# Shift and scale vectors of the first layer in quarters of 256 channels, x loaded ahead of the context

## The chip, the cores and the metric

The kernel runs on one core of one Trainium2 chip. The metric is the device time of one execution in microseconds (us), the median of several runs. Engines: TensorE (PE, matmuls; PEld, its weight loads), VectorE (DVE), ScalarE (ACT), GpSimd (POOL), and SP, which here only issues DMA transfers.

## What is computed

One hybrid layer (attention beside a Mamba-2 scan), one short-convolution layer, each followed by a SwiGLU, over 512 latent tokens `x` with 1024 channels, and 256 context tokens `ctx` that only layer 0 reads. All of it is float32. What matters here is the entry into layer 0:

```python
mod = (jax.nn.silu(c) @ ada_w[0] + ada_b[0])[:, None, :]
sh1, sc1, g1, sh2, sc2, g2 = jnp.split(mod, 6, axis=-1)
hx = modulate(rms_norm(x, norm_mix[0]), sh1, sc1)          # h * (1 + scale) + shift
mod_c = (jax.nn.silu(c_ctx) @ ada_w[0] + ada_b[0])[None, None, :]
csh1, csc1, ... = jnp.split(mod_c, 6, axis=-1)
hc = modulate(rms_norm(ctx, norm_mix[0]), csh1, csc1)
p_lat, p_ctx = hx @ w_in, hc @ w_in                        # keys, values, queries, ...
```

So the kernel needs, before any projection, the first two of the six parts of `ada_w[0]` (shift and scale, 1024 columns each, 8 MB together), for two vectors, `c` and `c_ctx`.

## The kernel before, in words

Activations lie with channels on the partitions: `xt` is 128 x 8 x 512, chunk k holding channels 128k to 128k+127. Every large product is made of three matmuls (`mm3`, lines 114 to 120) on values split into a high and a low half: `split` (line 92) lets ScalarE round to the high half and VectorE subtract for the low one.

`hybrid` (line 339) is the start. `load` issues ctx and x, two transfers each. `begin` makes the sums of squares (`stats`: squares on ScalarE, adds on GpSimd for ctx and VectorE for x, then matmuls with ones), the reciprocal root (`rsqrt`, nine small operations on VectorE), its broadcast over the partitions (`bcast`, matmuls, line 307) and the product with every chunk (line 366: GpSimd for ctx, VectorE for x). `both` on line 359 sets which of the two goes first.

`ada_first` (line 206) makes shift and scale with matmuls that fill only 32 of the array's columns each, four of them side by side ("strips", lines 198 to 204). It runs over four groups, each for one part and one half of the channels: shift of half 0, scale of half 0, shift of half 1, scale of half 1. Each group loads four tiles `adaw` of 512 KB, makes 16 strip matmuls into a `psS` tile, copies the result out on ScalarE (`strip_r`, line 222), and turns it by two matmuls with the constant `pick` (line 224) into columns; VectorE adds the bias (lines 228, 229) and, after a scale group, makes `gsc` and `cgsc` (lines 232, 233). Then the generator yields the half, and `hybrid` makes that half's four chunks (lines 382 to 384): ScalarE writes the high half `act_hi` or `hc_hi`, VectorE the full value `mod_u`, and VectorE (x) or GpSimd (ctx) the low half `act_lo` or `hc_lo`.

`jobs` runs `begin` after the first transfer of the first group and `weights` after the first transfer of the third group; `weights` issues and splits the first three tiles of the plan, the kv weights `w_kvd`.

`mixer` (line 388) then projects keys, values and dt (the kv matmuls, lines 406 to 415): for every chunk k six token groups, 0 and 1 of ctx, accumulated in one `psS` tile (`kvc`), 2 to 5 of x, in three `psA` tiles and one `psV` tile. 8 x 6 x 3 = 144 matmuls of 272 columns. The q projection follows (lines 429 to 437, 96 matmuls of 512 columns), then ten feature tiles, the rotary work and the masks on VectorE and GpSimd.

A planner orders each engine's instructions by priority and by its own idea of when they become ready; an engine then runs its list in order. `manual_schedule` holds an engine to the written order inside the block. `psS` has two buffers, `psA` three, `psV` one; `adaw` twelve; the weight tiles `wst`, `whi`, `wlo` three each.

## Time and profile before

| | us |
|---|---|
| median of 3 runs (lowest, highest) | 1289.33 (1287.85, 1292.81) |
| the profiled execution | 1291.26 |
| its span, first to last instruction | 1289.4 |
| TensorE busy in it | 1239.6 (96%) |
| VectorE busy | 729.4 (57%) |
| ScalarE busy | 448.4 (35%) |
| GpSimd busy | 179.5 (14%) |
| data moved by DMA | 158.52 MB, mean 123 GB/s |

A busy share is an average over the whole span. What a change at the start is worth is read from the first hundred microseconds: which wait ends last there. The chain of work that ended last is 83% TensorE.

### The profile page before, as it was taken

Reading aid. Unit: us, or ns where it says so; the run is one execution under the profiler, and the core shown is the slowest. Engines: PE = TensorE matmul, PEld = TensorE weight load, DVE = VectorE, ACT = ScalarE, POOL = GpSimd, SP = SyncE. Lnnn points to the kernel's source line nnn. Section 1 sums busy time; section 2 is a strip of 40 time slices with the busy share of each in tenths; the row PEclk is TensorE's granted clock in tenths of the full one; section 3 lists DMA queues with packets and bytes.
Section 4 is the critical chain, followed back from the end, with each engine's and each line's share of the span. In section 5 each row is a group of like instructions: output and inputs, shape, how many; then the busy total and the mean of one; then the engine's idle time right before and its main releaser. Section 6 shows DMA issues by size and latency. Waiting matters only on the chain.

```text
span 1289.4 us, 15875 instructions
## 1 busy us (share of the span) xinstructions
PE 1239.6 (96%) x6086; PEld 1021.6 (79%) x6086; DVE 729.4 (57%) x1187; ACT 448.4 (35%) x675; POOL 179.5 (14%) x199
## 2 busy tenths in 40 slices
PE   5998988899999999999999999999999999999997
PEld 3887765567898888888888988888988888888886
DVE  4898799985564777788422554443743333332223
ACT  3534534455353222223222342223532222222221
POOL 3423335440220000000000100002200000000001
PEclk9999989999999999999999999999999999999998
DMA  9331343300514777777333323333133333333322
GB/s 369 127 99 49 96 155 125 115 17 1 163 50 143 227 243 243 235 240 249 118 91 94 111 79 93 95 97 112 50 114 98 99 98 98 97 91 90 94 87 66
DMA packets 54845, 158.52 MB, mean 123 GB/s; under 512 B 6000, under 2 KB 8688, under 8 KB 54512
## 3 DMA queue, kind: packets, MB, share of 16 engines
q1 hardware_dynamic: 54480, 157.20, 38.1%
q8 instruction: 48, 0.79, 0.2%
q10 hardware_dynamic: 288, 0.31, 0.1%
q14 instruction: 29, 0.24, 0.1%
HBM read 154.86 MB, written 2.10 MB: 122 GB/s over the span
## 4 chain that ended last, share of the span: by engine, by line
PE 83%; DVE 9%; DMA 3%; issue 3%; POOL 1%; ACT 0%; SPq 0%; DVEq 0%; ACTq 0%; POOLq 0%
PE psS L116 14%; PE psS L117 14%; PE psS L118 14%; PE psA L116 10%; PE psA L118 10%; PE psA L117 10%; DVE xtok L257 2%; PE psV L830 2%; DMA adaw<-ada 2%; PE psS L961 1%; PE psS L822 1%; DVE mx L804 1%; DVE wlo L95 1%; PE psS L963 1%; DMA xT<-xT 1%
## 5 line engine op out<-in xcount | busy, mean ns | idle before, releaser
L95 DVE TENSOR_TENSOR wlo<-wst,whi 128x1024 fp32r<-128x1024 f32 (+2 forms) x194 | 235.0, 1214 | 315.2 <-ACT whi L94 312.3
L94 ACT CAST whi<-wst 128x1024 fp32r<-128x1024 f32 (+2 forms) x194 | 198.2, 1025 | 544.8 <-PE psS L117 242.1
L116 PE MATMUL psS<-act_hi,whi 128*128 128x512 f32 x760 | 297.0, 391 | 1.2 <-DVE cs_a L573 1.0
L117 PE MATMUL psS<-act_lo,whi 128*128 128x512 f32 x760 | 296.7, 390 | 0.0
L118 PE MATMUL psS<-act_hi,wlo 128*128 128x512 f32 x760 | 296.6, 390 | 0.0
L118 PEld LDWEIGHTS psS<-act_hi,wlo 128*128 128x128 f32 x760 | 143.1, 188 | 29.7
L116 PEld LDWEIGHTS psS<-act_hi,whi 128*128 128x128 f32 x760 | 143.0, 188 | 29.5 <-issue 1.2
L117 PEld LDWEIGHTS psS<-act_lo,whi 128*128 128x128 f32 x760 | 143.0, 188 | 27.9
L325 POOL TENSOR_TENSOR sq_acc<-sq_acc,sq 128x512 f32<-128x512 f32 (+1 forms) x28 | 38.0, 1356 | 872.5 <-issue 645.8
L116 PE MATMUL psA<-ffn_h_hi,whi 128*128 128x512 f32 (+1 forms) x396 | 145.3, 367 | 0.0
L118 PE MATMUL psA<-ffn_h_hi,wlo 128*128 128x512 f32 (+1 forms) x396 | 144.9, 366 | 0.0
L117 PE MATMUL psA<-ffn_h_lo,whi 128*128 128x512 f32 (+1 forms) x396 | 144.8, 366 | 0.0
L257 DVE SCALAR_TENSOR_TENSOR ada_acc<-ada_st,silu_c,ada_acc 128x512 f32<-128x512 f32 x98 | 73.4, 749 | 27.5 <-DMA ada_st<-ada 26.0
L117 PEld LDWEIGHTS psA<-ffn_h_lo,whi 128*128 128x128 f32 x396 | 74.7, 189 | 12.1
L116 PEld LDWEIGHTS psA<-ffn_h_hi,whi 128*128 128x128 f32 x396 | 74.7, 189 | 12.0
L118 PEld LDWEIGHTS psA<-ffn_h_hi,wlo 128*128 128x128 f32 x396 | 74.7, 189 | 12.0
L116 PE MATMUL psA<-act_hi,whi 128*128 128x512 f32 (+1 forms) x216 | 80.0, 370 | 0.0
L118 PE MATMUL psA<-act_hi,wlo 128*128 128x512 f32 (+1 forms) x216 | 79.2, 367 | 0.8 <-DVE wlo L95 0.8
L117 PE MATMUL psA<-act_lo,whi 128*128 128x512 f32 (+1 forms) x216 | 79.5, 368 | 0.0
L916 DVE SCALAR_TENSOR_TENSOR xT<-psA,mod,xT 128x512 f32<-128x512 f32 (+1 forms) x40 | 25.7, 643 | 68.2 <-PE psA L118 68.0
L94 ACT CAST ffn_h_hi<-sg 128x512 fp32r<-128x512 f32 x44 | 27.4, 622 | 59.1 <-DVE sg L980 59.1
L118 PEld LDWEIGHTS psA<-act_hi,wlo 128*128 128x128 f32 x216 | 40.8, 189 | 8.0 <-DVE wlo L95 1.3
(297 smaller groups left out, 1804.4 us busy)
## 6 DMA issues: line engine op xcount, KB each, us to landing
wst<-w_gu SPq DMA_DIRECT2D x88, 512.0 KB, 3.6
ada_st<-ada SPq DMA_DIRECT2D x112, 256.0 KB, 4.0
wst<-w_dn SPq DMA_DIRECT2D x32, 512.0 KB, 3.5
wst<-ada SPq DMA_DIRECT2D x24, 512.0 KB, 3.8
wst<-w_sc SPq DMA_DIRECT2D x24, 512.0 KB, 3.6
adaw<-ada SPq DMA_DIRECT2D x16, 512.0 KB, 10.4
wst<-w_dn SPq DMA_DIRECT2D x16, 384.0 KB, 3.2
wst<-w_f SPq DMA_DIRECT2D x10, 512.0 KB, 3.6
```

What stands on the lines that cost most here:

```text
L94: nc.scalar.copy(hi, src)
L95: nc.vector.tensor_tensor(lo, src, hi.bitcast(F32), ALU.subtract)
L116: nc.tensor.matmul(out, lhsT=a[0], rhs=b[0], start=start, stop=False)
L117: nc.tensor.matmul(out, lhsT=a[0], rhs=b[1], start=False, stop=False)
L118: nc.tensor.matmul(out, lhsT=a[1], rhs=b[0], start=False, stop=stop)
L257: nc.vector.scalar_tensor_tensor(a, w[:, i], c, a, ALU.mult, ALU.add)
L325: nc.gpsimd.tensor_tensor(self.acc[:, ts], self.acc[:, ts], sq, ALU.add)
L804: nc.vector.tensor_reduce(mx[:, c:c + 1], s[:, 0:768], AX.X, ALU.max)
L822: nc.tensor.matmul(s[:, a * T:a * T + T], lhsT=kt[x][:, ks], rhs=q[x], start=(x == 0), stop=(x == 1))
L830: nc.tensor.matmul(av, lhsT=vz[:, kc, vs], rhs=e[:, a], start=(c + a == 0), stop=(c + a == CHUNKS - 1))
L916: nc.vector.scalar_tensor_tensor(xt[:, d, ts], ps, gate[:, d:d + 1], xt[:, d, ts], ALU.mult, ALU.add)
L961: nc.tensor.matmul(out, lhsT=a[:, k * P:(k + 1) * P], rhs=hi, start=(k == 0 and a is w[0]), stop=False)
```

## The change

`ada_first` now runs over eight groups, each for one part and one quarter (256 channels, two chunks). A group loads two tiles of 512 KB from a new input `ada_first`, which holds the same weights in another layout, four chunks of the inner dimension by 256 columns each. The four strips now stand for four chunks of the inner dimension instead of two chunks by two column halves, so `pick` has two columns and adds four strips up. The strip matmuls are held to the written order on TensorE. After each scale group a quarter is yielded, and its two chunks are made.

Further: x comes before ctx in `both`, in `load` and in the kv matmuls' inner loop; the three kv weights are issued one by one, after the groups 1, 3 and 5; and SP is held to the written order until the last chunk is made.

```diff
@@ -195,43 +195,39 @@
     def psS(self):
         return self.ps.tile([P, 1024], F32, name="psS", tag="S", bufs=2)
 
-    def strips(self, ps, w, lhsT, first, last):
-
-        for i in range(2):
-            for h in range(2):
-                g = 32 * (2 * i + h)
-                self.nc.tensor.matmul(ps[g:g + 32, 0:256], lhsT=lhsT[i], rhs=w[:, i, 256 * h:256 * h + 256],
-                                      start=first, stop=last)
-
     def ada_first(self, pool, jobs):
+
         nc, t = self.nc, self.t
         scw = pool.tile([P, KC, 2, 16], F32, name="silu_w")
         for v in range(2):
             nc.vector.tensor_copy(scw[:, :, v, :], self.sc[:, v, :, None].broadcast_to([P, KC, 16]))
         scw = scw.rearrange("p k v r -> p k (v r)")
-        for n, j in enumerate((0, 2, 1, 3)):
-            part, half = j // 2, j % 2
+        for n in range(8):
+            quarter, part = n // 2, n % 2
             ps = self.psS()[:, 0:512]
-            for q in range(4):
-                w = pool.tile([P, 2, 512], F32, name="adaw", tag="adaw", bufs=12)
-                nc.sync.dma_start(out=w, in_=t["ada"][0, j, :, 2 * q:2 * q + 2, :])
-                if (n, q) in jobs:
-                    jobs[n, q]()
-                self.strips(ps, w, [scw[:, 2 * q + i] for i in range(2)], q == 0, q == 3)
+            for e in range(2):
+                w = pool.tile([P, 4, 256], F32, name="adaw", tag="adaw", bufs=12)
+                nc.sync.dma_start(out=w, in_=t["ada_first"][part, quarter, e])
+                if (n, e) in jobs:
+                    jobs[n, e]()
+                with self.tc.manual_schedule(engines={mybir.EngineType.PE}):
+                    for i in range(4):
+                        nc.tensor.matmul(ps[32 * i:32 * i + 32, 0:256], lhsT=scw[:, 4 * e + i], rhs=w[:, i],
+                                         start=(e == 0), stop=(e == 1))
             r = pool.tile([P, 256], F32, name="strip_r", tag="strip_r", bufs=2)
             nc.scalar.copy(r, ps[:, 0:256])
             for x in range(2):
-                nc.tensor.matmul(ps[:, 256 + x:264:2], lhsT=r[:, x * P:(x + 1) * P], rhs=self.con("pick", 4),
+                nc.tensor.matmul(ps[:, 256 + 2 * x:258 + 2 * x], lhsT=r[:, x * P:(x + 1) * P], rhs=self.con("pick", 2),
                                  start=True, stop=True)
-            hs = slice(4 * half, 4 * half + 4)
-            b = self.vec("ada_b", 4 * j, 4)
-            nc.vector.tensor_tensor(self.mod[:, 0, part, hs], ps[:, 256:260], b, ALU.add)
-            nc.vector.tensor_tensor(self.cmod[:, part, hs], ps[:, 260:264], b, ALU.add)
+            ks = slice(2 * quarter, 2 * quarter + 2)
+            b = self.vec("ada_b", 8 * part + 2 * quarter, 2)
+            nc.vector.tensor_tensor(self.mod[:, 0, part, ks], ps[:, 256:260:2], b, ALU.add)
+            nc.vector.tensor_tensor(self.cmod[:, part, ks], ps[:, 257:260:2], b, ALU.add)
             if part == 1:
-                g = self.vec("norm_mix", 4 * half, 4)
-                nc.vector.scalar_tensor_tensor(self.gsc[:, 0, 0, hs], self.mod[:, 0, 1, hs], 1.0, g, ALU.add, ALU.mult)
-                nc.vector.scalar_tensor_tensor(self.cgsc[:, hs], self.cmod[:, 1, hs], 1.0, g, ALU.add, ALU.mult)
-                yield half
+                g = self.vec("norm_mix", 2 * quarter, 2)
+                nc.vector.scalar_tensor_tensor(self.gsc[:, 0, 0, ks], self.mod[:, 0, 1, ks], 1.0, g, ALU.add, ALU.mult)
+                nc.vector.scalar_tensor_tensor(self.cgsc[:, ks], self.cmod[:, 1, ks], 1.0, g, ALU.add, ALU.mult)
+                yield quarter
 
     def ada_rest(self, pool, layer, parts, acc=None, bufs=2, tag=None):
         nc, t = self.nc, self.t
@@ -356,7 +352,7 @@
                 nc.scalar.copy(rb, self.bcast(r, n // P)[0])
                 return rb
 
-            both = ((ct, TC, nc.gpsimd), (xt, T, nc.vector))
+            both = ((xt, T, nc.vector), (ct, TC, nc.gpsimd))
 
             def begin():
                 rows = [self.stats(sp, a, n, eng=eng) for a, n, eng in both]
@@ -366,13 +362,14 @@
                         eng.tensor_tensor(a[:, k], a[:, k], rb, ALU.mult)
 
             def weights():
-                for i in range(3):
-                    self.ready.append(self.weight(*self.plan[i]))
-
+                self.ready.append(self.weight(*self.plan[len(self.ready)]))
+
+            order = tc.manual_schedule(engines={mybir.EngineType.SP})
+            order.__enter__()
+            load(xt, "xT")
             load(ct, "ctxT")
-            load(xt, "xT")
-            for half in self.ada_first(sp, {(0, 0): begin, (2, 0): weights}):
-                for k in range(4 * half, 4 * half + 4):
+            for quarter in self.ada_first(sp, {(0, 0): begin, (1, 1): weights, (3, 1): weights, (5, 1): weights}):
+                for k in range(2 * quarter, 2 * quarter + 2):
                     for a, n, eng in both:
                         x = a is xt
                         g, s = (self.gsc[:, 0, 0], self.mod[:, 0, 0]) if x else (self.cgsc, self.cmod[:, 0])
@@ -382,6 +379,7 @@
                         nc.scalar.activation(hi, halved(a[:, k]), AF.Identity, bias=s[:, k:k + 1], scale=g[:, k:k + 1])
                         nc.vector.tensor_scalar(u, a[:, k], g[:, k:k + 1], s[:, k:k + 1], ALU.mult, ALU.add)
                         eng.tensor_tensor(lo, halved(u), hi.bitcast(F32), ALU.subtract)
+            order.__exit__(None, None, None)
         with tc.tile_pool(name="mix", bufs=1) as mp:
             return self.mixer(mp, h, hc, hcp)
 
@@ -411,7 +409,7 @@
             wv = [a[:, :544].rearrange("p (a b) -> p a b", a=2) for a in w]
             for i in range(2):
                 k = 2 * q + i
-                for c in range(CHUNKS):
+                for c in (2, 3, 4, 5, 0, 1):
                     self.mm3(kv[c], hc.tok(k, c) if c < 2 else h.tok(k, c - 2), [wv[0][:, i], wv[1][:, i]], k == 0, k == KC - 1)
         ssk = pp.tile([P, CHUNKS, 2], F32, name="ssk")
         ssq = pp.tile([P, 4, 8], F32, name="ssq")
@@ -1092,6 +1090,8 @@
     s = f["sc_w_in"][0]
     a["w_sc"] = np.stack([_tiles(s[:, q * D:(q + 1) * D], P) for q in range(3)], axis=1)
     a["w_so"] = _tiles(f["sc_w_out"][0], P)
+    first = f["ada_w"][0][:, :2 * D].reshape(2, 4, P, 2, 4, 256)
+    a["ada_first"] = first.transpose(3, 4, 0, 2, 1, 5)
     a["ada"] = np.stack([_tiles(f["ada_w"][l], 512) for l in range(2)])
     parts = [_cols(f["c"]), _cols(f["c_ctx"]), _cols(f["ada_b"]), _cols(f["norm_mix"]), _cols(f["norm_ffn"]),
              _cols(f["final_norm"]), _cols(f["hy_conv_w"][0]), _cols(f["hy_conv_b"]),
@@ -1107,9 +1107,8 @@
     con[:, 0:128] = np.eye(P)
     con[:, 128:256] = 1.0
     con[:, 256:384] = q[:, None] % 32 == q[None, :] % 32
-    for g in range(4):
-        for v in range(2):
-            con[32 * g + 16 * v, 384 + 2 * v + g % 2] = 1.0
+    for v in range(2):
+        con[16 * v::32, 384 + v] = 1.0
     at = CAT[1]
     con[:, at:at + 128] = le
     con[:, at + 128:at + 256] = ge
```

## Rows read from the trace of the kernel before

**Rows 1.** The page: busy tenths in 40 slices of 32.2 us, granted clock, DMA share

```profile
PE   5998988899999999999999999999999999999997
DVE  4898799985564777788422554443743333332223
PEclk9999989999999999999999999999999999999998
DMA  9331343300514777777333323333133333333322
```

**Rows 2.** Stretches: us; busy us (instructions) per engine; PEclk, DMA share, GB/s

```profile
7.00:21.00 14.00, 8.07 (x43) 6.26 (x44) 6.76 (x22) 6.80 (x14) 4.05 (x6) 1.00 1.02 415
21.00:35.40 14.40, 12.03 (x120) 6.23 (x119) 10.62 (x27) 4.78 (x10) 6.00 (x8) 1.00 1.02 393
36.40:39.80 3.40, 3.40 (x21) 2.35 (x21) 3.40 (x7) 2.94 (x6) 3.21 (x3) 0.60 0.42 170
39.80:57.10 17.30, 17.30 (x141) 16.73 (x140) 14.77 (x28) 8.57 (x15) 8.54 (x9) 1.00 0.18 52
57.10:79.10 22.00, 22.00 (x98) 17.89 (x97) 19.95 (x72) 7.48 (x19) 4.08 (x8) 1.00 0.41 123
52.70:101.10 48.40, 45.09 (x239) 38.18 (x237) 45.21 (x117) 17.94 (x37) 19.68 (x24) 0.99 0.31 95
101.10:104.60 3.50, 3.43 (x12) 2.96 (x13) 3.50 (x4) 0.90 (x2) 3.50 (x4) 0.59 0.00 0
104.60:160.00 55.40, 53.24 (x277) 43.03 (x276) 41.03 (x80) 27.51 (x55) 16.63 (x33) 1.00 0.27 78
```

**Rows 3.** Timeline of SP: start, us, queue, line, transfer, count

```profile
2.77 11.54 SPq L217 DMA_DIRECT2D adaw<-ada  x9
...
15.26 2.89 SPq L108 DMA_DIRECT2D wst<-w_kvd  x3
19.10 7.02 SPq L217 DMA_DIRECT2D adaw<-ada  x7
```

**Rows 4.** DMA issues at 1.65 and near 25.8 us: size, us to landing

```profile
xT<-xT SPq DMA_DIRECT2D x1, 1024.0 KB, 8.5
...
adaw<-ada SPq DMA_DIRECT2D x1, 512.0 KB, 10.8
```

**Rows 5.** Timeline of VectorE, 20 to 53 us: start, us, what, count, [idle before]

```profile
22.16 0.67 DVE L150 SCALAR_TENSOR_TENSOR rs_y<-rs_t,rs_y 128x4 f32<-128x4 f32 x1
...
27.70 5.16 DVE L366 TENSOR_TENSOR xT<-xT,rb 128x512 f32<-128x512 f32 x8
...
34.23 0.16 DVE L232 SCALAR_TENSOR_TENSOR gsc<-mod,vecs 128x4 f32<-128x4 f32 x1
...
44.72 0.16 DVE L232 SCALAR_TENSOR_TENSOR gsc<-mod,vecs 128x4 f32<-128x4 f32 x1
...
50.80 1.82 DVE L384 TENSOR_TENSOR act_lo<-mod_u,act_hi 128x512 fp32r<-128x512 f32 x2
```

**Rows 6.** Timeline of TensorE: x's broadcast, first q matmul, two waits near 100 us

```profile
25.11 1.32 PE L307 MATMUL psA<-cons,rs_y 128*128 128x128 f32 x8
...
57.11 0.40 PE L116 MATMUL psS<-whi,act_hi 128*128 128x512 f32 x1
...
99.48 0.66 PE L584 MATMUL psA<-cons,xf 128*128 128x128 f32 x4 [2.22 <-DVE xf L576]
101.17 0.76 PE L116 MATMUL psS<-act_hi,whi 128*128 128x512 f32 x1 [1.03 <-DVE cs_a L573]
```

**Rows 7.** Timeline of GpSimd: the normalisation of ctx

```profile
22.09 6.00 POOL L366 TENSOR_TENSOR ctxT<-ctxT,rb 128x256 f32<-128x256 f32 x8 [10.64 <-ACT rb L356]
```

**Rows 8.** Groups on GpSimd, 36 to 53 us: busy us, mean ns, idle before

```profile
L384 POOL TENSOR_TENSOR hc_lo<-mod_u,hc_hi 128x256 fp32r<-128x256 f32 x8 | 8.6, 1095 | 14.8 <-ACT hc_hi L382 14.5 <-DVE mod_u L383 0.3
```

**Rows 9.** Instructions on tile mod_u, 30 to 55 us: ns min/median/max, first and last start

```profile
L383 DVE TENSOR_SCALAR mod_u<-xT,gsc,mod x8: 535/542/959, 34.4 to 49.9; 128x512 f32<-128x512 f32 x8
...
L384 DVE TENSOR_TENSOR act_lo<-mod_u,act_hi x8: 679/884/1217, 36.9 to 51.9; 128x512 fp32r<-128x512 f32 x8
```

## The prediction

> **What bounds the kernel now.** I read the forty slices first [rows 1]. TensorE stands at nine tenths almost everywhere; the two places to look at are the first slice, where it does little and the DMA engines are full, and the stretch up to slice 9, where VectorE is at seven to nine tenths beside it. The change touches only what happens before the q projection, so I then read the early stretches one by one [rows 2]. From 7 to 35.4 us the DMA share is 1.02 at 393 to 415 GB/s: transfers bound this part. From 39.8 to 57.1 us TensorE is busy for all 17.3 us while DMA falls to 0.18: now the key and value (kv) matmuls bound. They could not start sooner, because the first scale vector (`gsc`) comes at 34.23 and the second at 44.72 [rows 5], each for half of the channels. The first q matmul is at 57.11 [rows 6]. From there to 101.1 VectorE is nearly full too (45.21 of 48.4 us between 52.7 and 101.1, rows of [rows 2]), and twice it holds TensorE up, 2.22 and 1.03 us [rows 6], after which the clock row falls to 0.59.
>
> So the end of the whole kernel moves by what the q projection's start moves, as far as VectorE lets it through. I work out the end of the kv matmuls, now 57.1.
>
> **The change, part by part.**
>
> *Quarters in place of halves.* The bytes are the same: sixteen transfers of 512 KB, with x, ctx and three kv weights among them. The last of the seven late ones is issued near 25.8 us (19.10 + 7.02 less its own issue) and lands 10.8 us later, at 36.5 [rows 3, 4]. I keep 36.5. The first quarter needs only four of the sixteen, so the first two kv chunks can start some 12 us before 35.4, and the last quarter holds back only two chunks of eight. In before, `gsc` trails the last landing by 8.2 us (36.5 to 44.72), since strips, copy and picks stand in order behind matmuls and VectorE work. Its bare work is about 2.3 us, an estimate from eight strips, a copy, two picks and four small adds of 0.16 us [rows 5]. Behind `gsc` came 7.9 us for four chunks (44.72 to 52.62, the end of the last `act_lo`) [rows 5], so 4.0 for two. Then TensorE's tail: 36 matmuls at most, at 17.30/141 = 0.123 us each [rows 2] 4.4 us, of which about half run beside VectorE: 2.2. The **DMA chain** thus ends between 36.5 + 2.3 + 4.0 + 2.2 = 45.0 and 50.9.
>
> *x ahead of ctx.* The first half of x lands at 10.2 (issued 1.65, 8.5 us) [rows 4]. Without ctx's 1 MB ahead of it that is 2.5 us earlier at 415 GB/s [rows 2]. Its broadcast now waits on TensorE from 22.83 to 25.11 behind strips [rows 5, 6]; if x's statistics lead, these 2.3 us go too. So x's normalisation starts not at 27.70 but at about 22.9; without the queue gain it is 25.2. ctx pays: its rows come after x's on ScalarE and VectorE, and GpSimd owes it 6.0 us of normalising and 8.6 us of `hc_lo` [rows 7, 8]. If its root (1.8 us) follows x's eight products (5.2 us) on VectorE, it starts near 30 instead of 22.09 and ends near 44.6, still ahead of VectorE below. The ctx accumulators also share the two buffers of `psS` with the eight strip groups, so ctx matmuls may queue until the seventh group is read, near 39; 36 + 36 matmuls at 0.123 us then end near 48. The new chunk order (x chunks first) lets TensorE do x meanwhile and costs nothing by itself.
>
> *VectorE, the real limit of the start.* From 27.70 to 52.62 it was busy 22.4 us (24.9 less the 2.5 idle in 39.8 to 57.1) [rows 2, 5]. Added are eight more small adds and four more products, 12 x 0.16 = 1.9 us at most; ctx's reciprocal root, nine small operations, may now fall into this time, 1.8 us; the first kv weight's split, 1.1 us. Part of this fits into the idle time before 23 us (VectorE was busy 6.76 of 14 us there [rows 2]); I charge about half, 2.3 of the 4.8. So VectorE ends at 22.9 + 22.4 + 2.3 = 47.6, with TensorE's last matmuls 1.9 behind: **49.5**. The durations hide a spread: the same `mod_u` took 0.535 to 0.959 us and `act_lo` 0.679 to 1.217 [rows 9], the long ones where GpSimd worked too. With all sixteen short, 9.7 us, with all long, 17.4; the medians' 11.4 lie nearer the short end. [...]
>
> *More instructions elsewhere.* Four more copies of the strips on ScalarE, and eight more picks of about 0.15 us on TensorE, 1.2 us: hidden under the transfers before 36 us, except the last pair, which is in the 2.3. If the cover went, they cost those 1.2 us. The strips themselves stay 64 matmuls of 256 columns.
>
> *Fixed order on SP.* In before the SP queue already issues ctx, x, nine strips' weights, three kv weights, seven more [rows 3], which is the written order, so this edit alone gives 0. Queued behind a waiting transfer would be the next kv weight and all later transfers; the thirteenth transfer needs the first of twelve buffers back, which its strips free long before. A later weight cannot overtake, and none has to.
>
> **What is late next.** The q projection starts 57.1 - 49.5 = 7.6 us earlier. It lasts 22.0 us on TensorE [rows 2], unchanged. VectorE has 19.95 us of work there, and in 52.7 to 101.1 only 3.2 us idle, so it gains 5.0 us (52.6 to 47.6) against TensorE's 7.6. The missing 2.6 us can come from work that nobody awaits yet: after 104.6 VectorE is idle 14.4 of 55.4 us [rows 2]. As the planner orders each engine by what is ready, I expect that to be moved and the gain to pass.
>
> **Sum.** The profiled execution took 1291.3 us, a span of 1289.4 and 1.9 around it; less 7.6 that is 1283.7. The median of the three runs is 1.9 lower, 1289.3, and on it the forecast is **1281.7**. The bounds are 45.0, and 49.5 + 2.3 = 51.8 where x's normalisation starts at 25.2: a gain of 5.3 to 12 us.
>
> **The rivals.**
>
> *Everything hidden, chance 0.15.* VectorE gets the short durations, the DMA chain binds: 45.0, a gain of 12, and the 3.3 us of waits near 100 us shrink too. That gives 1274 to 1278, say 1276. For it: VectorE idles half the time from 7 to 21 us. Against it: strips stood in line 8.2 us in before.
>
> *VectorE keeps the difference, 0.14.* If the idle work is not moved, TensorE gains only what VectorE gains, 3.1 (47.6 plus the 1.9 behind it) to 5.0 us: about 1285.5. For it: 45.21 busy of 48.4, and both waits near 100 us have VectorE as releaser.
>
> *GpSimd beside VectorE, 0.06.* ctx's 14.6 us on GpSimd now lie wholly beside x's sixteen operations. If all of these take their long times, VectorE ends 6.0 us later and the gain is 1.6: 1287.7. Against it: GpSimd worked beside most of them in before, and the medians are as they are. [...]
>
> [...]
>
> *ctx becomes the tail, slower, 0.08.* ctx's reciprocal root stands behind x's eight products and the first chunks on VectorE. From the normalisation of ctx on, GpSimd needs 14.6 us, and a few matmuls follow, 1.5 us. The point where it decides is 57.1 - 16.1 = 41: each microsecond that ctx starts later is lost. Started at 48, with x's later operations stuck behind ctx's on VectorE, it costs 7: 1296. Against it: nine operations of 0.2 us have to be late by 18 us over my 30.
>
> *It does not do what it says, 0.01.* The bytes before the last quarter are the same, and if the first quarters' kv matmuls wait in TensorE's order behind the last strips, nothing moves: 1289.
>
> **How the numbers follow.** The forecast case, 1279.5 to 1284.5, has 0.50. A measurement of this kernel tells about 0.5%, 6.4 us, from no change, so the line is 1282.9. Of the forecast's 0.50 three quarters lie below it, 0.37; with the hidden case's 0.15 that is faster 0.52. Same is 0.13 + 0.14 + 0.06 + 0.06 + 0.01 = 0.40. Slower is 0.08. The range runs from 1276 to 1288: it leaves out the slower case, half of the best one and part of the clock's.
>
> **What would show it.** The first kv matmul near 23 us instead of 35.4; x's normalisation near 23; the last `gsc` between 39 and 43; the last `act_lo` near 47.6; the first q matmul near 49.5; the waits near 100 us about 7 us earlier. [...]

## The result, and the profile after

The kernel after takes 1299.03 us (median of eight executions, 1294.36 to 1300.46) against 1291.38 us for the kernel before beside it: a ratio of 1.0058, 95% interval 1.0040 to 1.0077, slower by 0.6%. The forecast was 1281.7. The profiled execution of after took 1300.46 us, a span of 1298.7 where before had 1289.4. It is the slowest of the eight, so the 9.3 us between the spans are more than the 7.7 between the medians. What follows splits the 9.3 us, and three marks in the timeline of SP show where they arise: the first `cdup` transfer (the conv part is through), the first `w_gu` transfer (the mixer is nearly through), and the end.

The timeline of SP in before (start, us, queue, line, transfer):

```profile
143.46 2.44 SPq L701 DMA_DIRECT2D cdup<-cf  x4
340.87 9.50 SPq L108 DMA_DIRECT2D wst<-w_gu  x4
```

and in after:

```profile
147.47 2.44 SPq L699 DMA_DIRECT2D cdup<-cf  x4
350.26 9.59 SPq L108 DMA_DIRECT2D wst<-w_gu  x4
```

`cdup` is 4.0 us later, `w_gu` 9.4, and from there to the end both take the same (948.5 and 948.4 us). So **4.0 us are lost up to `cdup`**, in and behind the start that the change rewrites, and **5.4 more in the mixer's attention and SSD part**, where not a line was changed.

**The start.** VectorE's timeline in after, 24 to 55 us (start, us, line, what), against [rows 5]:

```profile
24.19 0.16 DVE L224 TENSOR_TENSOR mod<-psS,vecs 128x2 f32<-128x2 f32 x1 [1.93 <-PE psS L220]
24.27 7.01 DVE L362 TENSOR_TENSOR xT<-xT,rb 128x512 f32<-128x512 f32 x8
31.20 0.14 DVE L225 TENSOR_TENSOR cmod<-psS,vecs 128x2 f32<-128x2 f32 x1
...
32.38 0.68 DVE L228 SCALAR_TENSOR_TENSOR gsc<-mod,vecs 128x2 f32<-128x2 f32 x1
...
38.54 0.16 DVE L228 SCALAR_TENSOR_TENSOR gsc<-mod,vecs 128x2 f32<-128x2 f32 x1
...
44.37 0.16 DVE L224 TENSOR_TENSOR mod<-psS,vecs 128x2 f32<-128x2 f32 x1 [2.79 <-PE psS L220]
...
45.01 0.16 DVE L228 SCALAR_TENSOR_TENSOR gsc<-mod,vecs 128x2 f32<-128x2 f32 x1
...
50.33 0.16 DVE L224 TENSOR_TENSOR mod<-psS,vecs 128x2 f32<-128x2 f32 x1 [2.27 <-PE psS L220]
...
51.35 0.16 DVE L228 SCALAR_TENSOR_TENSOR gsc<-mod,vecs 128x2 f32<-128x2 f32 x1
...
53.11 1.28 DVE L381 TENSOR_TENSOR act_lo<-mod_u,act_hi 128x512 fp32r<-128x512 f32 x2
```

The first scale vector could have come at 25: both strip groups of the first quarter were picked by then. But the eight products of x stand between its `mod` and its `cmod`, so `gsc` comes at 32.38, hardly sooner than the 34.23 of before. After it each quarter takes another 6.2 to 6.5 us, a **ladder** to 51.35, and VectorE waits for TensorE's picks on it (2.79, 2.27). TensorE's timeline shows the other side:

```profile
31.45 3.40 PE L215 MATMUL psS<-adaw,silu_w 128*32 128x256 f32 x32 [5.39 <-issue]
34.78 0.39 PE L116 MATMUL psA<-whi,act_hi 128*128 128x272 f32 x1
...
39.28 1.93 PE L215 MATMUL psS<-adaw,silu_w 128*32 128x256 f32 x32
...
43.76 0.95 PE L220 MATMUL psS<-cons,strip_r 128*128 128x2 f32 x8
...
45.25 1.93 PE L215 MATMUL psS<-adaw,silu_w 128*32 128x256 f32 x32
...
51.12 0.29 PE L116 MATMUL psS<-whi,hc_hi 128*128 128x272 f32 x1
...
60.17 0.40 PE L116 MATMUL psS<-whi,act_hi 128*128 128x512 f32 x1
```

The strips of the second quarter wait 5.39 us, until `cmod` at 31.20 gives a buffer of `psS` back (the profile names no releaser here; the strips start 0.1 us behind the end of that `cmod`). From then on TensorE works without a break, but in its list the kv matmuls of one quarter stand between the strips and the picks of the next: the strips of 39.28 are done at 41.2, their picks follow at 43.76. The strips of the last quarter run at 45.25, long after their data (last transfer issued at 26.58, median landing 9.7 us). ctx's kv matmuls come last, from 51.12, when `psS` has a buffer for them, and the first q matmul at 60.17 instead of 57.11 [rows 6]. The windows (us; busy us and instructions of TensorE, weight loads, VectorE, ScalarE, GpSimd; granted clock, DMA share, GB/s) say that from 35.4 on TensorE bounds this, and DMA no longer does:

```profile
21.00:35.40 14.40, 9.01 (x65) 6.54 (x58) 12.26 (x26) 4.18 (x8) 8.10 (x9) 1.00 1.03 403
35.40:57.10 21.70, 21.56 (x206) 19.18 (x205) 14.22 (x43) 12.38 (x23) 10.77 (x9) 1.00 0.12 39
```

Between 21 and 35.4 TensorE does 9.01 us of work where before it did 12.03 [rows 2]; behind that it is full, and the DMA share is 0.12.

Added up, TensorE has done 9.01 + 21.56 = 30.57 us of work from 21 to 57.1, where before has done 33.73. The 3.2 us that are missing are the 3.1 by which q starts later. On the ladder itself TensorE loses no time: from the first `gsc` to the last it is busy for 18.83 of 18.97 us. What it lost is the one wait of 5.39 us ahead of the ladder. The other 0.9 us up to `cdup` arise behind q's start, where the granted clock has a mean of 0.96 (60.17 to 147.47) instead of 0.98 in before (57.11 to 143.46).

**The mixer.** At one place of the attention and SSD part TensorE waits longer than in before for VectorE's row maximum `mx`. In after (TensorE, start, us):

```profile
256.45 1.01 PE L800 MATMUL psS<-kt,q 128*128 128x512 f32 x2 [2.36 <-DVE mx L802]
257.73 1.22 PE L777 MATMUL psA<-lx,xtok 128*128 128x256 f32 x2 [0.27 <-DVE xf L782]
...
260.46 0.63 PE L820 MATMUL psS<-q,kt 128*128 128x512 f32 x1
```

and the same place in before:

```profile
250.86 0.61 PE L802 MATMUL psS<-kt,q 128*128 128x512 f32 x2 [0.82 <-DVE mx L804]
252.14 0.70 PE L779 MATMUL psA<-lx,xtok 128*128 128x256 f32 x2 [0.67 <-DVE xf L784]
```

2.36 against 0.82 us, and behind it a matmul of 512 columns takes 0.63 us instead of 0.40, at a granted clock of 0.50 from 256.45 to 263 (it was 1.00 from 252.5 to 254). (A second wait for `mx`, 20 us later, is as long in before: 1.76 and 1.70 us.) VectorE's own rows there, in after:

```profile
251.42 1.52 DVE L253 SCALAR_TENSOR_TENSOR xtok<-wst,silu_c,xtok 128x512 f32<-128x512 f32 x1
252.87 1.21 DVE L95 TENSOR_TENSOR wlo<-wst,whi 128x1024 fp32r<-128x1024 f32 x1
254.00 1.52 DVE L253 SCALAR_TENSOR_TENSOR xtok<-wst,silu_c,xtok 128x512 f32<-128x512 f32 x1
255.45 0.94 DVE L802 TENSOR_REDUCE mx<-psS 128x1 f32<-128x768 f32 x1
```

A weight split that nobody awaits (`wlo`, 1.21 us) stands ahead of `mx`. In before that split comes behind this `mx`:

```profile
249.85 0.95 DVE L804 TENSOR_REDUCE mx<-psS 128x1 f32<-128x768 f32 x1
...
255.81 1.23 DVE L95 TENSOR_TENSOR wlo<-wst,whi 128x1024 fp32r<-128x1024 f32 x1
```

No line of the kernel says so: the planner ordered VectorE's work anew for the whole mixer, and the two lists differ there in many more places than this one. Why it chose another order is not shown; one may suppose that its own idea of the time at the end of the start was another.

### The profile page after: what moved, and what is told of

Same layout as the page of the kernel before. It is cut to its first block, busy times and chain, and to the rows that moved or that the text cites. A ratio compares the mean times of both kernels' runs of the same rounds, so it can differ in the third digit from the quotient of the medians.

```text
span 1298.7 us, 15937 instructions
## 1 busy us (share of the span) xinstructions
PE 1244.3 (96%) x6102; PEld 1027.9 (79%) x6102; DVE 731.9 (56%) x1199; ACT 450.4 (35%) x679; POOL 186.3 (14%) x199
## 4 chain that ended last, share of the span: by engine, by line
PE 82%; DVE 12%; issue 3%; POOL 1%; DMA 1%; ACT 1%; DVEq 0%; POOLq 0%; ACTq 0%
PE psS L116 14%; PE psS L118 14%; PE psS L117 14%; PE psA L118 10%; PE psA L116 10%; PE psA L117 10%; DVE xtok L253 2%; PE psV L828 2%; DVE mx L802 1%; PE psS L959 1%; DVE wlo L95 1%; PE psS L820 1%; PE psS L961 1%; PE psA L294 1%; PE psA L303 1%
## 5 line engine op out<-in xcount | busy, mean ns | idle before, releaser
L116 PEld LDWEIGHTS psS<-act_hi,whi 128*128 128x128 f32 x760 | 143.0, 188 | 29.3 <-issue 1.2
L94 ACT CAST ffn_h_hi<-sg 128x512 fp32r<-128x512 f32 x44 | 27.3, 621 | 58.4 <-DVE sg L978 58.4
```

The source lines that it names most:

```text
L94: nc.scalar.copy(hi, src)
L116: nc.tensor.matmul(out, lhsT=a[0], rhs=b[0], start=start, stop=False)
```

## The experiments

Sixteen kernels, each compared with before on the same chip. The table shows for each the first and last `gsc`, the first `cdup`, the time from there to the first `w_gu`, which of the two orders VectorE has in the mixer (P as in before, Q as in after; but for a few neighbours that change places, no third occurs), the median time, and the ratio of the times to before. The columns of `gsc`, `cdup` and the way to `w_gu` are us of the profiled execution. "Theory" and "rival" are names that the expectations give to explanations.

| kernel | first, last gsc | cdup | to w_gu | order | median us | ratio, 95% |
|---|---|---|---|---|---|---|
| before | 34.2, 44.7 | 143.5 | 197.4 | P | 1291.4 | |
| after | 32.4, 51.4 | 147.5 | 202.8 | Q | 1299.0 | 1.0040 to 1.0077 |
| e1 | 25.2, 47.6 | 146.4 | 197.2 | P | 1293.8 | 1.0008 to 1.0027 |
| e2 | 32.6, 56.5 | 148.2 | 197.1 | P | 1295.2 | 1.0018 to 1.0045 |
| e3 | 26.9, 49.1 | 145.8 | 198.0 | Q | 1294.3 | 1.0019 to 1.0052 |
| e4 | 33.1, 52.2 | 152.7 | 202.0 | Q | 1304.7 | 1.0061 to 1.0118 |
| e5 | 31.0, 51.1 | 147.1 | 199.0 | P | 1295.1 | 1.0014 to 1.0036 |
| e6 | 34.0, 60.6 | 155.1 | 197.1 | P | 1306.3 | 1.0087 to 1.0136 |
| e7 | 27.1, 56.3 | 148.9 | 196.9 | P | 1297.4 | 1.0033 to 1.0064 |
| e8 | 26.6, 59.7 | 155.5 | 199.1 | P | 1301.6 | 1.0053 to 1.0100 |
| e9 | 30.3, 54.6 | 152.7 | 197.6 | Q | 1304.9 | 1.0072 to 1.0131 |
| e10 | 27.3, 50.3 | 154.0 | 202.4 | Q | 1305.5 | 1.0073 to 1.0124 |
| e11 | 34.1, 48.3 | 154.9 | 197.5 | P | 1302.3 | 1.0065 to 1.0095 |
| e12 | 33.8, 47.9 | 155.0 | 199.4 | Q | 1307.0 | 1.0095 to 1.0141 |
| e13 | 33.8, 44.1 | 144.0 | 199.1 | P | 1292.7 | 0.9993 to 1.0018 |
| e14 | 29.9, 48.3 | 143.0 | 202.1 | Q | 1294.0 | 1.0013 to 1.0039 |
| e15 | 33.7, 41.6 | 146.4 | 199.1 | P | 1295.6 | 1.0012 to 1.0039 |
| e16 | 33.8, 41.7 | 144.1 | 198.3 | Q | 1293.2 | 1.0000 to 1.0030 |

### Which part of the change costs the start: e1 to e4

e1, the products of x one by one inside the loop over quarters, VectorE in written order:

```diff
-                    for k in range(KC):
-                        eng.tensor_tensor(a[:, k], a[:, k], rb, ALU.mult)
+                    rbs[n] = spread(ss, n)
...
-            order = tc.manual_schedule(engines={mybir.EngineType.SP})
+            order = tc.manual_schedule(engines={mybir.EngineType.SP, mybir.EngineType.DVE})
...
+                        eng.tensor_tensor(a[:, k], a[:, k], rbs[n], ALU.mult)
```

> The changed kernel, but x's and ctx's products with the reciprocal root stand in the loop over the quarters, and VectorE is held to the written order through the start, so that no more than two products of x can come ahead of a quarter's scale vector. In the changed kernel the first scale vector comes at 32.4 us, the last at 51.4, the first q matmul at 60.2. Theory 1 (the block of eight products on VectorE, 7.0 us, stands ahead of the first group's adds, and those hold the psS buffer that the third group's strips wait for): first scale vector at 24 to 26, q start at 53 to 55. Theory 2 (a ladder: with two psS buffers and TensorE's in-order list each quarter costs 6.3 us, whatever VectorE does): first scale vector at 24 to 26 too, but still 6.3 us from one to the next, so the last at 43 to 45. If the ladder is no limit, the last at 39 to 41. Theory 4 (most of the loss arises after the q projection, where the planner made other lists): q start earlier by 5, the total by anything between 0 and 10.

e2, both strip groups of a quarter in one `psS` tile, 512 columns each:

```diff
-            ps = self.psS()[:, 0:512]
+            if part == 0:
+                bank = self.psS()
+            ps = bank[:, 512 * part:512 * part + 512]
```

> The changed kernel, but shift and scale of a quarter share one psS tile (its two halves), so that four tiles instead of eight pass through the two buffers. Theory 1 (block of products): first scale vector still near 32, q start earlier by at most 2. Theory 2 (ladder of psS buffers): the strips of the next quarter no longer wait for this quarter's adds; from one scale vector to the next 3.5 to 5 us instead of 6.3, last one at 43 to 47, q start at 54 to 57. If neither holds, all stays at 60.2.

e3, the quarters without x's lead (ctx first again, in the loads, the loop and the kv chunks):

```diff
-            both = ((xt, T, nc.vector), (ct, TC, nc.gpsimd))
+            both = ((ct, TC, nc.gpsimd), (xt, T, nc.vector))
...
-                for c in (2, 3, 4, 5, 0, 1):
+                for c in range(CHUNKS):
```

> The changed kernel with ctx ahead of x again in the loads, in the statistics and products, and in the kv matmuls; quarters and order of SP kept. Theory 3 (x ahead of ctx is at fault, since ctx's products then run on GpSimd beside x's on VectorE and make them 7.0 instead of 5.2 us): q start at 55 to 58, total below the changed kernel's by 3 or more. Theories 1 and 2: x's products start near 27 instead of 24.3, the first scale vector comes at 32 to 34, q start at 60 to 62, total not below the changed kernel's.

e4, x's lead without the quarters, on before:

```diff
-            both = ((ct, TC, nc.gpsimd), (xt, T, nc.vector))
+            both = ((xt, T, nc.vector), (ct, TC, nc.gpsimd))
...
-                for c in range(CHUNKS):
+                for c in (2, 3, 4, 5, 0, 1):
```

> The kernel before with x ahead of ctx alone (loads, statistics and products, kv matmuls); halves and everything else kept. Theory 3: q start later than 57.1, total above the kernel before by 3 or more. Theories 1 and 2: x's products start near 24 instead of 27.7 and the first scale vector at 31 to 32 instead of 34.2, with no longer ladder, so q start at 54 to 57 and a total of 1283 to 1290. Theory 4: q start moves by a few us and the total by several us in either direction, apart from it.

In e1 the block is gone and the first `gsc` comes at 25.24, seven us sooner than in after. All that it brings at `cdup` is 1.1 us, because the ladder goes on, in steps of 8.5, 7.2 and 6.6 us:

```profile
25.24 0.16 DVE L228 SCALAR_TENSOR_TENSOR gsc<-mod,vecs 128x2 f32<-128x2 f32 x1
...
33.77 0.49 DVE L228 SCALAR_TENSOR_TENSOR gsc<-mod,vecs 128x2 f32<-128x2 f32 x1
...
40.94 0.50 DVE L228 SCALAR_TENSOR_TENSOR gsc<-mod,vecs 128x2 f32<-128x2 f32 x1
...
47.55 0.67 DVE L228 SCALAR_TENSOR_TENSOR gsc<-mod,vecs 128x2 f32<-128x2 f32 x1
```

From 21 to 57.1 TensorE does 34.67 us of work in e1, more than the 33.73 of before: without the block TensorE's loss in the start is gone. But little of that reaches `cdup`. q's first matmul stands at 53.00, among those of kv, which last to 60; and at 64.41 TensorE waits 1.50 us for q's next split weight (`wlo`). Nor does e1 tell whose work sets the steps: from the first `gsc` to the last TensorE is busy for 20.88 and VectorE for 20.17 of 22.31 us. e3 loses least (2.35 us at `cdup`), e4 most (9.3): without the quarters, x's lead makes the last `gsc` 7.5 us later. So x's lead costs in both pairs (147.5 against 145.8, 152.7 against 143.5), and the quarters alone, e3, gain nothing either. Arranging the buffers by the quarter, e2, made the ladder longer (steps of 8.5, 6.3 and 9.2 us, where 3.5 to 5 were expected of theory 2).

### The mixer's order alone: e5

After, without the two lines that hold SP's transfers in order:

```diff
-            order = tc.manual_schedule(engines={mybir.EngineType.SP})
-            order.__enter__()
...
-            order.__exit__(None, None, None)
```

> The kernel after, without the two lines that hold SP's transfers to the written order. SP's own list stays the same, and VectorE's list in the start keeps its block of eight products ahead of the first scale vector; but the planner then happens to give VectorE, in the attention and SSD part, the list of the kernel before. Theory 'list' (part of the loss is the mixer's other VectorE list and the half clock that follows its wait): the conv end (first cdup transfer) stays near 147, 4 later than before, but from there to the first w_gu transfer it takes 197 to 198 as in before, not 202.8; time 1294 to 1296. Rival 'start' (the mixer is only late because its start was late): the list changes nothing, 202 to 203 for that stretch, time 1298 to 1300.

SP's list is the same, transfer by transfer, as the forecast had it. The start stays as slow as in after. But VectorE's order in the mixer falls back to P, the stretch takes 199.0 us (197 to 198 were expected), and the median goes from 1299.0 to 1295.1:

```profile
147.09 2.45 SPq L696 DMA_DIRECT2D cdup<-cf  x4
346.09 9.29 SPq L108 DMA_DIRECT2D wst<-w_gu  x4
```

So about half of the loss hangs on the order that the planner happens to choose some 100 us behind `cdup`, as theory "list" had it. The other kernels of the table complete this. Each of the eight with order Q has the wait of 2.4 us for `mx` at this place, each of the ten with order P one of 0.3 to 0.8. And the eight fall into two groups. In after, e4, e10 and e14 the granted clock falls behind that wait, to means of 0.77 to 0.89 over 15 us, and the stretch takes 202.0 to 202.8 us. In e3, e9, e12 and e16 it stays at 1.00, and the stretch takes 197.6 to 199.4, hardly more than with order P (196.9 to 199.1). The same window in after and in e12 (105 to 120 us behind `cdup`):

```profile
252.50:267.50 15.00, 12.37 (x40) 8.41 (x39) 12.19 (x22) 5.82 (x10) 4.95 (x5) 0.77 0.33 105
```

```profile
260.00:275.00 15.00, 11.97 (x51) 8.54 (x50) 14.71 (x24) 6.95 (x12) 6.56 (x7) 1.00 0.34 106
```

51 matmuls where after has 40. The times suggest that this differs between executions of one kernel too (seven of e3's ten took 1293.35 to 1294.56, three 1299.04 to 1300.80), but only one execution of each has a trace.

The wait itself is about 1.5 us longer than in before. What the lower clock costs is an estimate from the stretches. Over 160 to 340 us the mean granted clock is 0.95 in after, e4, e10 and e14, and 0.97 to 0.98 in the other four of order Q; the 202.0 to 202.8 us of the first stand 2.6 to 5.2 above the 197.6 to 199.4 of the others. Not all of this need lie behind the wait, since the clock falls in other places of the stretch too. The ten kernels of order P show it: all have 1.00 over the 15 us at this place, yet the stretch takes 199.0 to 199.1 us with a mean of 0.96 over 160 to 340 (e5, e8, e13, e15) and 196.9 to 197.5 with 0.97 to 0.98 (the other six), 1.5 to 2.2 less. In after the first 100 us behind `cdup` lose no more to the clock than in before: the means are 0.97 and 0.95.

### Buffers: e6 to e12

e6, four groups side by side in a tile of `psS`; e7, the same on e1; e8, the same with x's products fused into the scaling:

```diff
-            ps = self.psS()[:, 0:512]
+            if n % 4 == 0:
+                bank = self.psS()
+            ps = bank[:, 256 * (n % 4):256 * (n % 4) + 256]
...
```

```diff
...
+                        if x:
+                            nc.vector.scalar_tensor_tensor(u, a[:, k], g[:, k:k + 1], rbs[n], ALU.mult, ALU.mult)
+                            nc.scalar.activation(hi, halved(u), AF.Identity, bias=s[:, k:k + 1])
+                            nc.vector.scalar_tensor_tensor(lo, halved(u), s[:, k:k + 1], hi.bitcast(F32), ALU.add, ALU.subtract)
...
```

> The kernel after, with the strips' accumulators of four groups (two quarters) side by side in one psS tile, so that no strip waits for a buffer. Theory 'buffers' (two psS buffers make the ladder of 6.3 us per quarter): the last gsc comes at 45 or sooner instead of 51.35, the first cdup transfer at 143 or sooner, time 1287 to 1291. Rival 'order' (TensorE's list has the later strips and picks behind the kv matmuls of earlier quarters, whatever the buffers): the last gsc stays between 48 and 53, the first cdup transfer near 146 to 147, time 1293 to 1296.

> The same four groups per tile, and x's products inside the loop over quarters with VectorE in written order: neither a block of products ahead of the first scale vector nor a wait for a buffer. Theory 'buffers and block' (these two are the whole loss of the start): first gsc near 25, last near 40 to 43, first cdup transfer at 139 to 141, time 1285 to 1288. Rival 'order' (TensorE's list): last gsc near 47 to 50, first cdup transfer at 145 to 147, time 1292 to 1295. If TensorE is without idle time from 26 to 57 and the end is still not earlier than before, TensorE's own sum of work was the limit.

> Four groups per tile, and x's eight products fused into the scaling (one operation times gsc times the root, and the shift added in the next), so that VectorE has eight 128x512 operations less, 5.2 to 7.0 us. Theory 'VectorE is the limit of the start', as I forecast: the first cdup transfer comes 4 to 7 us sooner than with four groups per tile alone, near 139 to 142, time 1285 to 1289. Rival 'order' (VectorE waits for TensorE's picks anyway): no more than 1 to 2 us sooner, time 1292 to 1295.

All three made the ladder longer, and in e6 and e7 the last `gsc` lies outside every range that was expected. They don't test the theory, since they put in a new wait: a strip group now waits for VectorE's read of its neighbour in the same tile. In e6 the strips waited 10.2 us for `cmod`, from the view of tile `adaw`:

```profile
  DVE cmod L227: 10.2, 6
```

Eight long operations less on VectorE (e8) don't bring `cdup` forward either: 155.5 against e6's 155.1. That speaks against VectorE as the limit while the strips are late, and doesn't settle it: the medians, 1301.6 and 1306.3, lie 4.7 us apart all the same, and the traces can't say why, since the profiled execution is the slowest of e8's four and the fastest of e6's.

e9 to e12 exchange the PSUM tiles instead, so that groups have buffers of their own and ctx needn't wait: e9 on after, e10 on e1, e11 on before, e12 on before with x's kv chunks first.

```diff
-            ps = self.psS()[:, 0:512]
+            ps = self.psA()
...
-        kvl = [self.psA() for _ in range(3)] + [self.psV()]
-        kvc = self.psS()
-        kv = [kvc[:, 0:272], kvc[:, 512:784]] + [p[:, 0:272] for p in kvl]
+        kvx, kvc = self.psS(), self.psS()
+        kvl = [kvx[:, 0:512], kvx[:, 512:], self.psA(), self.psV()]
+        kv = [kvc[:, 0:272], kvc[:, 512:784]] + [p[:, 0:272] for p in kvl]
```

> The kernel after with the PSUM tiles exchanged: the strips use the three one-bank buffers of psA, and the accumulators of four of the six token chunks, ctx's two among them, use psS. So ctx's kv matmuls needn't wait until the seventh strip group is read, and the block of eight products holds back no strip. Theory 'buffers': ctx's first kv matmul comes near 38 instead of 51.12, the last gsc at 45 or sooner, the first cdup transfer 3 to 5 us sooner than after's 147.47. Rival 'TensorE's sum': kv still starts only near 34 behind the block, and from there TensorE has some 18 us of kv matmuls (144 of 0.125), 6 us of strips and 3 of picks to do in any order, so that kv can't end before 58: the first cdup transfer at 145 to 147. The mixer's VectorE list is that of after, so 198 to 203 us follow from there to the first w_gu transfer; time 1293 to 1298.

> The same exchange of PSUM tiles, with x's products inside the loop over quarters and VectorE in written order (so kv starts near 29.5). Theory 'buffers': last gsc near 41 to 44, end of kv near 53, first cdup transfer at 139 to 141, 3 us sooner than before's 143.46. Rival 'TensorE's sum': TensorE is without idle time from 26 on, and 27 us of strips, picks and kv matmuls from there end near 54 at the earliest; with copies, picks and the written order's waits between them, near 56 to 58: first cdup transfer at 143 to 146. The mixer's VectorE list is that of after; time 1289 to 1298 by its clock.

> The kernel before with the same exchange of PSUM tiles alone: halves, ctx first, VectorE's mixer list as in before. If the buffers held the start of before up, the first cdup transfer comes 1 to 3 us sooner than 143.46 and the time falls to 1288 to 1290; if TensorE's sum of work sets the end, it stays within 1 us and the time within 1290 to 1293. The q projection may lose up to 2 us, since its accumulators now wait until the keys and values are read.

> As the one before, and the kv matmuls take x's four chunks ahead of ctx's two. Nothing else is written differently, but the planner now gives VectorE, in the mixer, the list of the kernel after. Theory 'list': the first cdup transfer within 1.5 us of the kernel with ctx's chunks first, but from there to the first w_gu transfer 198 to 203 us instead of 197 to 198, and in some executions 5 to 6 us on top from the half clock; time 1 to 7 us above that kernel. Rival 'start': the time differs by no more than the first cdup transfers do.

In e9 ctx's kv matmuls do start at 35.18 instead of 51.12, and the steps of the ladder grow, to 9.1, 7.7 and 7.5 us: twelve ctx matmuls more per quarter, 1.5 us at the full clock, stand between two `gsc` (the mean granted clock from 35.4 to 57.1 is 0.94). Theory "buffers" falls. In e10 the last picks run at 45.0, but VectorE in written order reaches the last `gsc` only at 50.30. In all four the q projection then waits 3.3 to 5.4 us for the kv accumulators to be read (e10):

```profile
PE psS L116 <- DVE dt L426: 5.4, 1, 5.4
```

That wait, and in e11 and e12 a last `gsc` 3.6 and 3.2 us later than in before, come with the exchange itself, so the times of these four say nothing on the change. e11 and e12 are one more pair for the mixer: with `cdup` at 154.9 and 155.0, order P and Q, their medians are 1302.3 and 1307.0.

### Whose work is the ladder: e13 and e14

One of the three products of each kv matmul (high part of the activations by low part of the weights) is left out, 48 of 144 matmuls; e13 on before, e14 on after:

```diff
-                    self.mm3(kv[c], hc.tok(k, c) if c < 2 else h.tok(k, c - 2), [wv[0][:, i], wv[1][:, i]], k == 0, k == KC - 1)
+                    a = hc.tok(k, c) if c < 2 else h.tok(k, c - 2)
+                    nc.tensor.matmul(kv[c], lhsT=a[0], rhs=wv[0][:, i], start=k == 0, stop=False)
+                    nc.tensor.matmul(kv[c], lhsT=a[1], rhs=wv[0][:, i], start=False, stop=k == KC - 1)
```

> The kernel before, and its kv matmuls leave out one of their three products (high part of the activations by low part of the weights): 48 of 144 matmuls less, so keys and values are less exact. Theory 'TensorE's sum' (from 21 us on TensorE has 33.7 us of work and 2.4 of idle time, and that sets the end of kv): 48 x 0.123 = 5.9 us less work bring the first cdup transfer 4 to 6 us sooner than 143.46, time 1285.5 to 1287.5. Rival 'chain' (the last gsc and VectorE's work behind it set the end, as my forecast had it): the last act_lo ends at 52.6 as before, kv not before 54.5, so no more than 2.6 us sooner, time 1289 or more.

> The same product left out of the kernel after. Theory 'TensorE's sum': again 4 to 6 us sooner than after's 147.47, time 1293 to 1295. Theory 'ladder' (each quarter waits for the strips and picks of the one before on TensorE, whose list has them behind kv matmuls): eight kv matmuls of 24 less per quarter shorten each of the three later steps of 6.3 by up to 1 us, and the backlog of ctx after 51 by 1.5: 4 to 5 sooner as well. Rival 'chain' (VectorE and the strips' way through psS alone): gsc keeps its steps of 6.3 us, only the matmuls behind the last one are fewer, 1 to 2.6 us sooner, time 1296 to 1298.

In after it brings 4.5 us at `cdup`. The two later steps of the ladder fall from 6.5 and 6.3 to 5.36 us each, but the first grows, from 6.2 to 7.6:

```profile
29.93 0.68 DVE L228 SCALAR_TENSOR_TENSOR gsc<-mod,vecs 128x2 f32<-128x2 f32 x1
...
37.54 0.16 DVE L228 SCALAR_TENSOR_TENSOR gsc<-mod,vecs 128x2 f32<-128x2 f32 x1
...
42.90 0.16 DVE L228 SCALAR_TENSOR_TENSOR gsc<-mod,vecs 128x2 f32<-128x2 f32 x1
...
48.26 0.16 DVE L228 SCALAR_TENSOR_TENSOR gsc<-mod,vecs 128x2 f32<-128x2 f32 x1
```

The fall is that of eight matmuls of 0.125 us, the number that x's four token groups of one quarter lose: the kv matmuls themselves are what these `gsc` wait for. For the two later steps theory "ladder" is shown. In the first, VectorE's two `act_lo` take 2.35 us instead of 1.28, and TensorE waits 1.16 us for them ahead of the picks.

The ladder is not where most of the gain comes from. q starts 5.5 us sooner (54.66 against 60.17): 2.45 because the first `gsc` comes sooner, at 29.93 (the eight products start at 22.35 instead of 24.27), 0.6 from the three steps together, and 2.4 from less work behind the last `gsc`.

In before, where kv and strips interleave too but only once, the same edit brings nothing (`cdup` 144.0). Theory "TensorE's sum" alone falls for it. Before and e13, 35.4 to 57.1 us:

```profile
35.40:57.10 21.70, 21.70 (x167) 20.07 (x165) 19.17 (x37) 12.50 (x22) 11.75 (x12) 0.92 0.25 86
```

```profile
35.40:57.10 21.70, 19.02 (x122) 16.56 (x119) 19.45 (x35) 12.04 (x23) 12.33 (x13) 0.79 0.27 86
```

Of 5.9 us less work 2.7 turn into idle time, and the rest is eaten by a granted clock of 0.79 instead of 0.92. Most of the idle time is one wait for GpSimd's low halves of ctx, so with less work on TensorE the next limit stood close behind:

```profile
48.61 0.59 PE L417 MATMUL psS<-whi,hc_lo 128*128 128x272 f32 x1 [1.81 <-POOL hc_lo L384]
```

### Could before have gained from earlier scale vectors: e15 and e16

e15 holds TensorE in before to the written order from the third strip group to the end of kv; e16 leaves out the product as well (edit of e13):

```diff
+            if n == 2:
+                self.order = self.tc.manual_schedule(engines={mybir.EngineType.PE})
+                self.order.__enter__()
             part, half = j // 2, j % 2
...
+        self.order.__exit__(None, None, None)
         ssk = pp.tile([P, CHUNKS, 2], F32, name="ssk")
```

> The kernel before, with TensorE held to the written order from the third strip group to the end of kv: the second half's strips and picks stand ahead of all kv matmuls, not between them. The last gsc can then follow the last landing (36.5) by about 2.5: near 39 to 40 instead of 44.72, and VectorE's last act_lo ends near 47 to 48 instead of 52.62. Theory 'two limits' (leaving out 5.9 us of kv matmuls moved nothing, so the chain of scale vectors is one limit; TensorE's own work is the other, close behind): kv can't start before some 38 and needs 18 us at the full clock, so the first q matmul comes at 56 to 57.5 and the first cdup transfer within 1 us of 143.46; time 1290 to 1293. Theory 'chain alone': the end follows the scale vectors, first q matmul near 52, first cdup transfer near 139, time 1286 to 1288.

> The same, and the kv matmuls leave out one of their three products (high part of the activations by low part of the weights). Theory 'two limits': now both are moved, and the first q matmul comes 4 to 6 us sooner than before's 57.11, near 51 to 53, the first cdup transfer near 138 to 140; where each edit alone gave nothing. Theory 'neither' (VectorE's work or the weights' way set the end): within 1.5 us of before. The planner gives VectorE the mixer list of the kernel after here, so the time is 1287 to 1294 and the transfers tell more than the time.

In e15 the last `gsc` comes at 41.59 instead of 44.72 (39 to 40 were expected) and the last `act_lo` ends at 49.50, 3.1 us sooner (47 to 48). But TensorE can't begin kv before 39.52 and then has it all to do:

```profile
39.52 0.37 PE L116 MATMUL psS<-whi,hc_hi 128*128 128x272 f32 x1
...
59.30 0.40 PE L116 MATMUL psS<-whi,act_hi 128*128 128x512 f32 x1
```

19.8 us, at a mean granted clock of 0.91 (from 40.2 to 43.1 the matmuls of 272 columns start 0.23 us apart, from 43.7 on 0.13), and q starts 2.2 later than in before. My 56 to 57.5 took the full clock from 38 on; 0.91 of 19.8 us are its 18. `cdup`, at 146.4, is 2.9 us later than in before, where "two limits" had it within 1. The direction is that of "two limits"; "chain alone" falls. In e16 both are moved, and q's first matmul does come at 53.29, as forecast. The next one waits:

```profile
53.29 0.40 PE L116 MATMUL psS<-whi,act_hi 128*128 128x512 f32 x1
56.29 0.50 PE L117 MATMUL psS<-wlo,act_hi 128*128 128x512 f32 x1 [2.60 <-DVE wlo L95]
```

q's weights are not split yet, since VectorE's list has other work ahead of the split (from 49.69 to 54.75, most of it for the masks). This is a third limit, 0.8 us ahead of where q started in before. Behind the wait the granted clock falls, to a mean of 0.83 from 53.29 to 60 (a matmul of 512 columns takes 0.63 us from 57.92 on, 0.40 at 57.34). `cdup` comes at 144.1. "Neither" had this in its condition, and it is what was measured.

## Why the prediction was wrong

**The path.** The step that failed is the choice of the limit: the sum took VectorE for it and gave TensorE only the last matmuls behind it. VectorE's work had nearly the forecast size (23.50 us busy between 24.27 and 54.39, against 22.4 + 2.3). But the sum has no wait of VectorE for TensorE, and there 6.6 us of waits came, all for picks (2.79 and 2.27 the longest); the last `act_lo` ended at 54.39 instead of 47.6. The "1.9 behind" for TensorE's last matmuls has no row: in before 4.5 us lie between the end of the last `act_lo` and q, in after 5.8. So the limit from 31.45 on was TensorE, which has the small steps and the bulk in one list.

**The DMA chain.** "Its bare work is about 2.3 us" failed for the same reason. I read the 8.2 us from the last landing to the last `gsc` in before as something quarters would shed. They were largely kv matmuls ahead of strips and picks in TensorE's list. The last strips and picks of before stand between kv matmuls that run from 35.37 on:

```profile
40.19 0.64 PE L203 MATMUL psS<-adaw,silu_w 128*32 128x256 f32 x8
...
43.75 0.50 PE L224 MATMUL psS<-cons,strip_r 128*128 128x4 f32 x4
```

Quarters make that list alternate four times instead of twice. Measured: `gsc` 25 us behind the last issue, the last strips 45.25, the last `gsc` 51.35 instead of 39 to 43. The forecast looked at TensorE's order only in its last rival, with 0.01, and the other way round: kv matmuls behind the last strips.

**TensorE's sum.** No term of the sum was TensorE's whole work. From 21.0 to 57.1 before has

```profile
21.00:57.10 36.10, 33.73 (x283) 26.31 (x283) 29.79 (x62) 17.28 (x31) 17.75 (x20) 0.95 0.56 208
```

33.73 us busy of 36.10. At the rates of that trace, and unless some of this work is moved ahead of 21, 21.0 + 33.7 = 54.7 is the earliest end; the forecast 49.5 lies 5.2 us below it, and [rows 2] already show nearly all of this work. (In after TensorE was busy for 8.68 us from 7 to 21, 0.6 more than in before.) "About half run beside VectorE" for the tail looked at 36 matmuls and forgot the other 108.

**x ahead of ctx.** The products started at 24.27, within my 22.9 to 25.2. I had not asked where the planner would put them: all eight ahead of the first `cmod`, 7 us, with the second quarter's strips behind that. And they took 7.01 us, not 5.16: GpSimd's normalisation of ctx now ran beside them, from 26.55 to 34.60 (the last part has the comparison). Behind this block came the wait of 5.39 us, the one stretch of TensorE's time that the start lost; no term of the sum has it.

**ctx.** "ctx matmuls may queue until the seventh group is read, near 39" was the right mechanism. The seventh group was read at 50.40, and ctx's matmuls started at 51.12: a size that followed from the missing ladder. The slower rival named ctx as the tail, but for another reason (its reciprocal root), and its condition, a start after 41, was not met.

**More instructions elsewhere, hidden.** The eight more picks stand in the ladder, 0.95 us a quarter in the trace of after. The cover that I named, the transfers before 36, was gone by then.

**The fixed order on SP, 0.** Right for SP's queue and wrong for the price. Taking the lines away moves the median by about 4 us, through VectorE's order in the mixer.

**What is late next.** "I expect that to be moved and the gain to pass" was the second step that failed. In e16, where q could start at 53.29, its weights were split only at 56, and the gain stopped there; and the planner doesn't only move work that nobody awaits out of the way, it also moved a split ahead of a `mx` that TensorE awaits. The two waits near 100 us came at 102.24 and 103.93, 2.8 us later and not 7 sooner, and the loss of 4.0 us at `cdup` became 9.4 at `w_gu`.

**The clock.** The chances hold 0.06 for TensorE's clock, and the range a part of it. No run shows this term: in the start of after the granted clock was 1.00, in the mean of 21.00 to 35.40 as of 35.40 to 57.10. It fell in the mixer, to 0.77 in the mean of 252.50 to 267.50, where I had no rival.

What stays open: what a start without the block could gain at `cdup`. The trace of after puts the 3.1 us by which q starts later down to the wait behind the block; but without the block only 1.1 us come back at `cdup` (e1), without x's lead 1.7 (e3), and the two were not tried together. That the clock falls behind the 2.4 us wait in some kernels' traces and not in others is shown; what decides it is not. Nor is it shown why the planner's order changes. None of the sixteen kernels is faster than before.

## What to carry to other kernels

Before you split a stage into finer steps, add up the whole work of each engine in it, from the trace, and lay the result beside the chain: here TensorE's 33.7 of 36.1 us left 2.4 us to gain, unless work could be moved ahead of the stage. Then write down, for the engine that does both the small steps and the bulk, in what order they stand in its one list: finer steps pay only if each small step gets ahead of the bulk of the one before, and not even then where that engine's work fills the stage (e15). And where a planner orders the instructions, compare its lists far behind the edit too; another order there cost this kernel about as much as the edited stage itself.

## What the runs showed of the hardware

The eight products on VectorE took 5.16 us in before. The first, which GpSimd's normalisation of ctx (22.09 to 28.09) still overlaps, took 0.94 us, the seven behind it 0.68 each. In after they took 7.01 us: the four ahead of GpSimd's start at 26.55 took 0.68 to 0.69 each, the four that run beside it 1.20 to 1.21. GpSimd's own eight took 6.00 us in before (median 0.73) and 8.05 in after (median 1.17). So in these traces both took longer where they ran side by side; why, no run here shows. This cost stood in no term of my sum.

In each of the eight kernels of order Q TensorE waits 2.4 us for `mx` between matmuls that fill most of the time (12.0 to 12.4 of the 15 us at this place). In after, e4, e10 and e14 the granted clock has a mean of 0.77 to 0.89 over these 15 us, in the other four 1.00. In after it was 1.00 from 252.5 to 254, 0.50 from the end of the wait, at 256.45, to 263, and 1.00 from 263.5 on. The stretch from `cdup` to `w_gu` is 2.6 to 5.2 us longer in the four with the lower clock, not all of which need belong to this place. What decides between the two no run here shows.
